# Conditioning rows moved to other stages of a two-layer trunk, and the mixer's due jobs run sooner

## The chip, the core and the metric

The kernel runs on one core of a Trainium2 chip. The metric is the device time of one execution in microseconds (us), as the median over runs. The engines are named as in the profile: PE (TensorE, matrix products), DVE (VectorE), ACT (ScalarE), POOL (GpSimd) and SP (SyncE, whose queue issues most transfers).

## What is computed

The reference is a trunk of two layers over 1024 positions of width 1024, all in fp32. Layer 0 is a Griffin block followed by a squared-ReLU MLP; then one shared K/V is computed; layer 1 is chunked attention followed by an MLP of the same form. Each norm is modulated by shift and scale, and each residual is gated, by vectors that come from one conditioning vector `c` through the matrices `ada_w` (two layers, 6 x 1024 columns) and `kv_ada_w`:

```python
def modulate(x, shift, scale):
    return x * (1 + scale[:, None, :]) + shift[:, None, :]

def recurrent_mixer(hn, w_in, conv_w, conv_b, gate_a_w, gate_a_b, gate_x_w, gate_x_b, lam, w_out):
    z = hn @ w_in
    gate, xr = jnp.split(z, 2, axis=-1)
    xr = causal_depthwise_conv(xr, conv_w, conv_b)
    y = rg_lru(xr, gate_a_w, gate_a_b, gate_x_w, gate_x_b, lam)
    return (y * jax.nn.gelu(gate)) @ w_out

def sqrelu_mlp(hn, w1, w2):
    return jnp.square(jax.nn.relu(hn @ w1)) @ w2
```

## The kernel before

**Products.** Each fp32 operand is split into a high and a low part (fp32r), and a product is three matmuls (L329, L330, L331). ACT makes the high part (L196, tiles `wh`), DVE the low one by subtraction (L200, tiles `wl`, or `s` and the second half of `wh` for half tiles). The MLPs go by a scheme of seven products on quarters in place of eight; the weights' sums for it are made by DVE or POOL (L126), those of the hidden layer by DVE (L1182), and the sums of products by DVE: L1264 in the first product, L1286 in the second, which adds into the residual stream. A block of the first product and a step of the second are 84 matmuls each.

**Stream.** A class `Stream` plans the weight stream while the program is written. Items stand in a list; SP issues their loads (L159) in list order, into a ring of seven buffers (`ws`) or into general buffers (`s`). Items become operands in list order as buffers come free. Since each engine works in program order, this list and the moments at which the planner is asked (`ws.tick`, `ws.run`, which starts the jobs that have come due) set the order on every engine.

**Conditioning rows.** One row is an item of another kind: a load of 512 KB (128 x 1024 of `ada` or `kvada`) and on DVE one multiply-and-sum with the activated conditioning vector (L362, an instruction of its own and a short one that reads the sum). 72 rows after the first ones are dealt out one by one: `some(n)` in the mixer and beside the shared K/V (through the ring), `ada_late(n)` in the MLP of layer 0 (into general buffers). Nothing needs most of them before layer 1. The MLP of layer 1 has none.

**Stages, with times of the profiled execution.** Startup to 60; the mixer's loop over 11 tiles (to about 310), in which `some` gives rows at tiles 8, 9 and 10; out-projection in four pairs of w_out loads with four rows each (330 to 459), whose operands are the stored scan results (`ygd`); the out-projection's last part in chunks, with the squares (L541, L542) and normed parts (L605, L610, L620, L623) of the next norm as jobs (to 473); MLP of layer 0, first product in blocks q = 2 to 15 with two or three rows each (to 790), the hidden layer stored to DRAM (`hid`, issued by ACT) and loaded again, then the second product in steps (790 to 1143); K/V, attention, and layer 1's MLP (first product from 1714, second from 2026). In the trace `in_w_dram` stands for all weights whose names begin with w, `hsp` for the residual stream put aside in DRAM.

Of the kernel before, what the change touches and what calls it, by code (L numbers as in the profile page):

```python
# [27 lines left out]
def _done(t):  # L28

    return [b for b in range(W // BLK) if (b * BLK + BLK - 1) // 128 == t]  # L30
# [35 lines left out]
class Stream:  # L66
# [157 lines left out]
    def at(self, d, f, *a):  # L224

        if self.timed and d:
            self.jobs.append((self.now + d, f, a))
        else:
            f(*a)
# [74 lines left out]
def trunk(ctx: ExitStack, tc: tile.TileContext, I, out, dbg=None, stop=None):  # L304
# [16 lines left out]
    def bank(shape=(128, 512)):  # L321
        cnt[0] += 1
        return pools["b"].tile(list(shape), F32, name=f"b{cnt[0]}", tag="b")

    def hs(half):
        return slice(half * HALF, (half + 1) * HALF)
# [29 lines left out]
    ws = Stream(nc, slot, whp, wsp)  # L356
# [35 lines left out]
    def some(n):  # L392
        for _ in range(n):
            if rest:
                ws.add(*rest.pop(0))

    def gate_item(bs):
        for b in bs:
            if b % 4 == 0:
                ws.add(I["gates"][b // 4], 8 * BLK)  # L400

    def w_in(*us):
        for u in us:
            ws.add(I["w_in"][u], 1024)
# [6 lines left out]
    w_in(3)  # L411
    for t in range(4, NT):
        w_in(NT + t)
        some({8: 3, 9: 2, 10: 3}.get(t, 0))
        gate_item(_done(t - 1))
        w_in(t)
    gate_item(_done(NT - 1))
# [3 lines left out]
    def yg_items(n):  # L421
        for _ in range(n):
            k = len(ygits)
            ygits.append(ws.item([(0, S, ygd[k])], [(0, HALF, True), (HALF, HALF, True)], to="a",
                                 dep=k))

    def w_out(c, j):
        kn = 4 if c else 3
        ws.add(I["w_out"][c * 4 + j][:, : kn * 256], kn * 256)

    for j in range(4):
        if j == 0:
            yg_items(3)
        w_out(0, j)
        if j == 0:
            yg_items(4)
        w_out(1, j)
        some(4)
    yg_items(4)
    for j in range(4):  # L440
        w_out(2, j)
# [10 lines left out]
    def ada_late(n):  # L452
        for _ in range(n):
            if rest:
                src, _n, use = rest.pop(0)
                ws.item([(0, 1024, src)], [], to="u", raw=False, use=use)

    def hid_item(l, what):


        (p, nm), n = what[0], len(what)
        v, p = p, p % 16
        if n == 1:
            src = hid[p][:, HID.index(nm) : HID.index(nm) + 1]
        elif what[1][0] == v:
            i, d = HID.index(nm), HID.index(what[1][1]) - HID.index(nm)
            src = hid[p][:, i : i + d + 1 : d]
        else:
            src = hid[p : p + 2, :, HID.index(nm)].rearrange("a p b -> p a b")
        it = ws.item([(0, n * HALF, src)], [(x * HALF, HALF, True) for x in range(n)], to="a")  # L470
        for x, w in enumerate(what):
            hitems[(l, *w)] = (it, x)

    def mlp_units(l):
        for f in range(4):
            ws.add(I["w1"][l][f], 1024)
        for q in range(2, 16):
            u, v = I["w1"][l][2 * q], I["w1"][l][2 * q + 1]
            ws.add_quad(u[:, :512], u[:, 512:], v[:, :512], v[:, 512:], 512, V)
            ada_late(0 if l or q == 2 else 2 if q in (3, 15) else 3)  # L480
        for s in STEPS[: 16 if l else 15]:
            def quad(s):
                c = slice(s * 128, s * 128 + 512)
                ws.add_quad(*(I["w2"][l][s % 4][x][:, c] for x in range(4)), 512,
                            G if s > 1 else V)

            if s == 0:

                for nm in NAMES:
                    hid_item(l, [(0, nm), (1, nm)])  # L490
                    hid_item(l, [(2, nm), (3, nm)])
                    if nm == "B11":
                        quad(0)
            else:
                quad(s)
            if l or s < 14:
                if s < 15:
                    for nms in HLOADS:
                        hid_item(l, [(s + 4, nm) for nm in nms])
        if l == 0:  # L500
            for e in range(2):
                ws.add(I["w2t"][e], 1024)
            hid_item(l, [(18, "B11"), (18, "B12")])
            hid_item(l, [(18, "B22"), (18, "B21")])
            hid_item(l, [(16, "B12"), (17, "B12")])
            hid_item(l, [(15, "B12")])

    mlp_units(0)

    for g in range(2):  # L510
# [8 lines left out]
    for m in range(8):  # L519
        ws.add(I["wo"][m], 1024)  # L520
    mlp_units(1)


# [564 lines left out]
    def part_of(ps, it, e, half, ys, first, last):  # L1088

        n = len(ys)  # L1090
        for k, y in enumerate(ys):
            s = slice(k * 256 + e * 128, k * 256 + e * 128 + 128)
            gh, gl = y["op"][half]
            mm3(ps, it["hi"][:, s], it["lo"][:, s], gh, gl, first and k == 0, last and k == n - 1)

    def into_h(m, half, ps):
        V.scalar_tensor_tensor(out=h[m][:, hs(half)], in0=ps, scalar=g1[:, m : m + 1],
                               in1=h[m][:, hs(half)], op0=ALU.mult, op1=ALU.add)
# [23 lines left out]
    def chunk(j, half, e):  # L1122
        m, ps = 2 * j + e, bank()
        part_of(ps, its[j], e, half, ygits[7:], True, True)
        into_h(m, half, ps)
        at(int(m < KD - 1), n2.sq, m, hs(half), int(m < KD - 2))
# [5 lines left out]
            tick()  # L1132
    for j in range(4):
        for e in range(2):
            chunk(j, 1, e)
            n = 2 * j + e
            if n == 1:
                n2.mm(0)
            elif n == 3:
                n2.bc(0)  # L1140
            elif n > 3:
                n2.mod(0, (n - 4,))
            ws.tick()
        ws.done(its[j])
# [499 lines left out]
    for n in range(N + LAG + 1):  # L1644
        if n < N:
            hd, j = todo[n]
# [148 lines left out]
```

## Time and profile before

| | us |
|---|---|
| median of 3 runs | 2350.05 (2349.6 to 2352.07) |
| profiled execution | 2351.75 |
| its span | 2350.0 |
| granted clock of PE over the span | 0.99 |
| PE busy | 2258.7 (96%) |
| DVE busy | 1751.7 (75%) |
| ACT busy | 1246.2 (53%) |
| POOL busy | 397.1 (17%) |

A busy share is a mean over stages. Which engine holds the others up in one stage is read from the waits there: the time an engine stood idle before an instruction and what released it, which the timeline puts in brackets.

### The profile page before, as it was taken

To read this page: it belongs to the slowest core of one execution; us is meant where nothing else is said; L and a number is where in the kernel's file an instruction comes from. 1 tells how busy PE (TensorE), PEld (TensorE's weight loads), DVE (VectorE), ACT (ScalarE), POOL (GpSimd) and SP (SyncE) were. 2 spreads that over 40 slices of the span, in tenths; PEclk is the share of its full clock that TensorE was granted. 3 is DMA by queue.
4 is the path that set the end of the run, shared out by engine and by line. 5 is a ranking of instruction groups with operands and counts; after the bars stand their busy time and mean duration, and the time that the engine had idled before them with its cause. 6 is when DMAs were issued, how large, how long until landed. Compare 5 with 4: busy or idle time off the path is not lost.

```text
span 2350.0 us, 29512 instructions
## 1 busy us (share of the span) xinstructions
PE 2258.7 (96%) x10588; PEld 1871.9 (80%) x10588; DVE 1751.7 (75%) x2580; ACT 1246.2 (53%) x2148; POOL 397.1 (17%) x419
## 2 busy tenths in 40 slices
PE   4999989999999899999999989999999999999999
PEld 2878768878888678888888879997888888778887
DVE  8688887698787877777774759996496655877775
ACT  5587873375555634344443249995275555633332
POOL 0001100000000033331000068873000000033332
PEclk9999999999999999999999999999999999999999
DMA  8225466426666865445244200014114444865543
GB/s 316 72 83 153 121 208 214 176 68 237 245 249 235 305 232 158 152 151 207 84 159 126 90 12 10 11 53 148 64 58 160 171 165 168 297 232 160 157 150 128
DMA packets 141631, 363.32 MB, mean 155 GB/s; under 512 B 14924, under 2 KB 17100, under 8 KB 141484
## 3 DMA queue, kind: packets, MB, share of 16 engines
q1 hardware_dynamic: 113756, 278.45, 35.3%
q10 hardware_dynamic: 23824, 71.44, 8.1%
q0 software_dynamic: 3904, 11.54, 1.9%
q8 instruction: 83, 1.36, 0.2%
q14 instruction: 64, 0.52, 0.1%
HBM read 260.19 MB, written 89.65 MB: 149 GB/s over the span
## 4 chain that ended last, share of the span: by engine, by line
PE 68%; DVE 10%; DMA 10%; ACT 6%; issue 3%; POOL 2%; ACTq 0%; SPq 0%; POOLq 0%; DVEq 0%
PE b L329 21%; PE b L330 21%; PE b L331 21%; DMA hid<-s 4%; DMA ws<-in_w_dram 3%; DMA ws<-hid 2%; DVE wl L200 2%; PE b L1601 1%; ACT s L1571 1%; DVE s L200 1%; DVE s L1182 1%; ACT s L334 1%; POOL ws L126 1%; PE b L1620 1%; PE b L1621 1%
## 5 line engine op out<-in xcount | busy, mean ns | idle before, releaser
L329 PE MATMUL b<-s,wh 128*128 128x512 f32 (+1 forms) x2532 | 999.1, 395 | 29.6 <-DVE s L1286 11.0
L330 PE MATMUL b<-s,wh 128*128 128x512 f32 (+1 forms) x2532 | 994.6, 393 | 17.1 <-DVE s L200 8.5
L331 PE MATMUL b<-s,wl 128*128 128x512 f32 x2296 | 901.0, 392 | 1.7 <-DVE wl L200 1.7
L329 PEld LDWEIGHTS b<-s,wh 128*128 128x128 f32 (+1 forms) x2532 | 477.9, 189 | 144.2 <-DVE s L1286 8.5
L330 PEld LDWEIGHTS b<-s,wh 128*128 128x128 f32 (+1 forms) x2532 | 478.0, 189 | 124.3 <-DVE s L200 10.1
L196 ACT ACTIVATE wh<-ws 128x1024 fp32r<-128x1024 f32 (+3 forms) x302 | 291.4, 975 | 480.0 <-POOL ws L126 260.4
L331 PEld LDWEIGHTS b<-s,wl 128*128 128x128 f32 x2296 | 433.2, 189 | 95.9 <-DVE wl L200 2.5
L200 DVE TENSOR_TENSOR wl<-ws,wh 128x1024 fp32r<-128x1024 f32 (+1 forms) x249 | 304.3, 1224 | 156.5 <-ACT wh L196 154.2
L200 DVE TENSOR_TENSOR s<-ws,s 128x512 fp32r<-128x512 f32 x284 | 224.8, 807 | 7.4 <-ACT s L196 7.4
L1286 DVE SCALAR_TENSOR_TENSOR s<-b,mod,s 128x512 f32<-128x512 f32 x221 | 164.7, 746 | 86.4 <-PE b L331 86.3
L126 POOL TENSOR_TENSOR ws<-ws 128x512 f32<-128x512 f32 x21 | 27.8, 1322 | 1112.0 <-DVE s L1286 467.7
L196 ACT ACTIVATE s<-ws 128x512 fp32r<-128x512 f32 x284 | 164.4, 618 | 77.6 <-DMA ws<-hid 25.1
L330 PE MATMUL b<-wl,s 128*128 128x512 f32 x384 | 149.9, 390 | 0.0
L329 PE MATMUL b<-wh,s 128*128 128x512 f32 x384 | 148.9, 389 | 0.0
L331 PE MATMUL b<-wh,s 128*128 128x512 f32 x384 | 146.4, 389 | 1.1 <-DVE s L584 1.1
L1264 DVE TENSOR_TENSOR s<-s,b 128x512 f32<-128x512 f32 x84 | 57.3, 683 | 75.3 <-PE b L331 69.0
L362 DVE CUSTOM_DVE_ANT_0 ws<-ws,cb,vec 128x1024 f32<-128x1024 f32 x59 | 75.1, 1281 | 32.8 <-DMA ws<-in_ada_dram 26.1
L1262 ACT ACTIVATE s<-b 128x512 f32<-128x512 f32 x84 | 50.0, 595 | 89.7 <-PE b L331 87.5
L331 PE MATMUL b<-s,wh 128*128 128x512 f32 x236 | 92.5, 392 | 0.0
L335 DVE TENSOR_TENSOR s<-b,s 128x384 fp32r<-128x384 f32 x144 | 82.7, 593 | 12.1 <-ACT s L334 11.6
L1576 POOL TENSOR_SCALAR s<-s,sm 128x640 f32<-128x640 f32 (+4 forms) x128 | 86.1, 685 | 22.3 <-DVE sm L1574 22.3
L1571 ACT ACTIVATE s<-s,sm 128x640 f32<-128x640 f32 (+4 forms) x128 | 88.3, 696 | 1.6 <-DVE sm L1569 1.6
(165 smaller groups left out, 2980.7 us busy)
## 6 DMA issues: line engine op xcount, KB each, us to landing
hid<-s ACTq DMA_DIRECT2D x128, 512.0 KB, 4.9
ws<-hid SPq DMA_DIRECT2D x118, 512.0 KB, 4.9
ws<-in_w_dram SPq DMA_DIRECT2D x220, 256.0 KB, 3.6
ws<-in_ada_dram SPq DMA_DIRECT2D x56, 512.0 KB, 4.4
s<-in_ada_dram SPq DMA_DIRECT2D x40, 512.0 KB, 7.9
ws<-in_w_in_dram SPq DMA_DIRECT2D x22, 512.0 KB, 7.2
hsp<-s SPq DMA_DIRECT2D x32, 256.0 KB, 2.0
s<-hsp SPq DMA_DIRECT2D x16, 512.0 KB, 7.8
```

Of the source, the lines that this page charges most:

```text
L126: eng.tensor_tensor(out=out, in0=in0, in1=in1, op=op)
L196: self.nc.scalar.activation(out=hi[:rows, :n], in_=src, func=AF.Copy)
L200: self.nc.vector.tensor_tensor(out=lo[:rows, :n], in0=src, in1=hi[:rows, :n].bitcast(F32), op=ALU.subtract)
L329: PE.matmul(ps, ah, bh, start=start, stop=False, skip_group_check=more)
L330: PE.matmul(ps, ah, bl, start=False, stop=False, skip_group_check=more)
L331: return PE.matmul(ps, al, bh, start=False, stop=stop, skip_group_check=more).ins
L335: V.tensor_tensor(out=lo, in0=src, in1=hi.bitcast(F32), op=ALU.subtract)
L362: V.tensor_tensor_reduce(out=t, in0=t, in1=cb, op0=ALU.mult, op1=ALU.add, scale=1.0, scalar=bias, accum_out=dst)
L1264: V.tensor_tensor(out=t, in0=t, in1=ps, op=ALU.add)
L1286: V.scalar_tensor_tensor(out=t, in0=ps, scalar=g2[:, m : m + 1], in1=t, op0=ALU.mult, op1=ALU.add)
L1571: A_.activation(out=p[:, lo:640], in_=p[:, lo:640], func=AF.Exp, scale=-1.0, bias=m, accum_out=s1)
L1576: G.tensor_scalar(out=p[:, lo:640], in0=p[:, lo:640], scalar1=sm[:, 4 + e : 5 + e], scalar2=1.0, op0=ALU.mult, op1=ALU.mult)
```

## The change

Five edits. In the mixer's loop the eight rows stand with tiles 6, 7 and 8 in place of 8, 9 and 10. The out-projection's four pairs get 0, 5, 5 and 6 rows in place of four each. In the first product of layer 0's MLP the blocks q = 14 and q = 15 get no rows (they had three and two). In its second product the steps 4 to 11 get one row each. The mixer's last chunks run due jobs before each chunk. The number of rows is the same, so three fewer stand beside the shared K/V. Every line after L496 moves down by one, after L1135 by two.

```diff
--- before.py
+++ after.py
@@ -411,7 +411,7 @@
     w_in(3)
     for t in range(4, NT):
         w_in(NT + t)
-        some({8: 3, 9: 2, 10: 3}.get(t, 0))
+        some({6: 3, 7: 2, 8: 3}.get(t, 0))
         gate_item(_done(t - 1))
         w_in(t)
     gate_item(_done(NT - 1))
@@ -435,7 +435,7 @@
         if j == 0:
             yg_items(4)
         w_out(1, j)
-        some(4)
+        some((0, 5, 5, 6)[j])
     yg_items(4)
     for j in range(4):
         w_out(2, j)
@@ -477,7 +477,7 @@
         for q in range(2, 16):
             u, v = I["w1"][l][2 * q], I["w1"][l][2 * q + 1]
             ws.add_quad(u[:, :512], u[:, 512:], v[:, :512], v[:, 512:], 512, V)
-            ada_late(0 if l or q == 2 else 2 if q in (3, 15) else 3)
+            ada_late(0 if l or q in (2, 14, 15) else 2 if q == 3 else 3)
         for s in STEPS[: 16 if l else 15]:
             def quad(s):
                 c = slice(s * 128, s * 128 + 512)
@@ -493,6 +493,7 @@
                         quad(0)
             else:
                 quad(s)
+            ada_late(int(l == 0 and 3 < s < 12))
             if l or s < 14:
                 if s < 15:
                     for nms in HLOADS:
@@ -1132,6 +1133,7 @@
             tick()
     for j in range(4):
         for e in range(2):
+            ws.run()
             chunk(j, 1, e)
             n = 2 * j + e
             if n == 1:
```

DVE, out-projection's first pair, from the timeline's 348.76 on; `s<-ws` are lows of stored scan results, `wl` lows of w_out, L362 rows. Before:

```order
L200 TENSOR_TENSOR s_2391<-ws_2195,s_2391 128x512
L200 TENSOR_TENSOR s_2393<-ws_2195,s_2393 128x512
L362 ISA ws_2378,mod_82<-ws_2378,cb,vec 128x1024
L362 ISA mod_82 128x1
L200 TENSOR_TENSOR s_2395<-ws_2305,s_2395 128x512
L200 TENSOR_TENSOR s_2397<-ws_2305,s_2397 128x512
L1014 TENSOR_TENSOR s_2022<-s_2022,s_2284 128x1024
L362 ISA ws_2449,mod_82<-ws_2449,cb,vec 128x1024
L362 ISA mod_82 128x1
L1097 SCALAR_TENSOR_TENSOR s_2454<-b_2464,mod_82,s_2454 128x512
```

After:

```order
L200 TENSOR_TENSOR s_2391<-ws_2195,s_2391 128x512
L200 TENSOR_TENSOR s_2393<-ws_2195,s_2393 128x512
L200 TENSOR_TENSOR s_2395<-ws_2305,s_2395 128x512
L200 TENSOR_TENSOR s_2397<-ws_2305,s_2397 128x512
L200 TENSOR_TENSOR wl_2487<-ws_2351,wh_2486 128x768
L1015 TENSOR_TENSOR s_2022<-s_2022,s_2284 128x1024
L362 ISA ws_2448,mod_82<-ws_2448,cb,vec 128x1024
L362 ISA mod_82 128x1
L1098 SCALAR_TENSOR_TENSOR s_2453<-b_2463,mod_82,s_2453 128x512
L362 ISA ws_2484,mod_82<-ws_2484,cb,vec 128x1024
```

One row (its two instructions) has gone from between the lows, a second a few instructions ahead (`ws_2351`), and a low of w_out stands sooner.

DVE, second product, the step from 874 on. Before:

```order
L1286 SCALAR_TENSOR_TENSOR s_6367<-b_6433,mod_82,s_6367 128x512
L200 TENSOR_TENSOR s_6515<-ws_6380,s_6515 128x512
L1286 SCALAR_TENSOR_TENSOR s_6367<-b_6434,mod_82,s_6367 128x512
L200 TENSOR_TENSOR wl_6532<-ws_6428,wh_6531 128x1024
L200 TENSOR_TENSOR s_6534<-ws_6380,s_6534 128x512
L1286 SCALAR_TENSOR_TENSOR s_6367<-b_6435,mod_82,s_6367 128x512
```

After:

```order
L1288 SCALAR_TENSOR_TENSOR s_6352<-b_6418,mod_82,s_6352 128x512
L200 TENSOR_TENSOR s_6502<-ws_6365,s_6502 128x512
L1288 SCALAR_TENSOR_TENSOR s_6352<-b_6419,mod_82,s_6352 128x512
L362 ISA s_6442,kvmod<-s_6442,cb,vec 128x1024
L362 ISA kvmod 128x1
L200 TENSOR_TENSOR wl_6519<-ws_6413,wh_6518 128x1024
L200 TENSOR_TENSOR s_6521<-ws_6365,s_6521 128x512
L1288 SCALAR_TENSOR_TENSOR s_6352<-b_6420,mod_82,s_6352 128x512
```

A row stands behind the second L1286 (now L1288) of the step; seven later steps read alike.

SP, second product, one of the following steps. Before:

```order
L159 DMA ws_6726<-in_w_dram 128x512
L159 DMA ws_6731<-in_w_dram 128x512
L159 DMA ws_6754<-in_w_dram 128x512 x2
L159 DMA ws_6796<-hid 128x2x512
L159 DMA ws_6798<-hid 128x2x512
L159 DMA ws_6836<-hid 128x1024
```

After:

```order
L159 DMA ws_6717<-in_w_dram 128x512
L159 DMA ws_6722<-in_w_dram 128x512
L159 DMA ws_6745<-in_w_dram 128x512 x2
L159 DMA s_6748<-in_kvada_dram 128x1024
L159 DMA ws_6789<-hid 128x2x512
L159 DMA ws_6791<-hid 128x2x512
L159 DMA ws_6830<-hid 128x1024
```

The row's load stands behind the step's loads of w2 and ahead of those of the hidden layer.

DVE, mixer's end, the last normed parts ahead of the MLP. Before:

```order
L623 TENSOR_TENSOR s_3351<-s_2454,s_3351 128x512
L200 TENSOR_TENSOR wl_3355<-ws_2985,wh_3354 128x1024
L1097 SCALAR_TENSOR_TENSOR s_2503<-b_3383,mod_82,s_2503 128x512
L542 TENSOR_TENSOR s_3102<-s_3102,s_3398 128x512
L605 SCALAR_TENSOR_TENSOR s_2460<-s_2460,aa,s_2462 128x512
L542 TENSOR_TENSOR s_3102<-s_3102,s_3403 128x512
L542 TENSOR_TENSOR s_3102<-s_3102,s_3373 128x512
L623 TENSOR_TENSOR s_3376<-s_2456,s_3376 128x512
```

After:

```order
L624 TENSOR_TENSOR s_3337<-s_2453,s_3337 128x512
L200 TENSOR_TENSOR wl_3355<-ws_3007,wh_3354 128x1024
L543 TENSOR_TENSOR s_3102<-s_3102,s_3359 128x512
L543 TENSOR_TENSOR s_3102<-s_3102,s_3385 128x512
L1098 SCALAR_TENSOR_TENSOR s_2504<-b_3391,mod_82,s_2504 128x512
L543 TENSOR_TENSOR s_3102<-s_3102,s_3406 128x512
L606 SCALAR_TENSOR_TENSOR s_2459<-s_2459,aa,s_2461 128x512
L624 TENSOR_TENSOR s_3362<-s_2455,s_3362 128x512
```

Two sums of squares (L542, now L543) stand ahead of the last addition into the stream (L1097, now L1098) in place of behind it, and one normed part (L623, now L624) comes closer to it.

## Rows read from the trace of the kernel before

**Rows 1.** The page's first part: busy time of each engine, share, instructions.

```profile
PE 2258.7 (96%) x10588; PEld 1871.9 (80%) x10588; DVE 1751.7 (75%) x2580; ACT 1246.2 (53%) x2148; POOL 397.1 (17%) x419
```

**Rows 2.** Timeline, PE: start, us, engine, line, operation, count [idle before <-releaser].

```profile
342.56 0.50 PE L330 MATMUL b<-s,wh 128*128 128x512 f32 x1 [1.81 <-DVE s L200]
...
349.47 0.79 PE L330 MATMUL b<-s,wh 128*128 128x512 f32 x1 [5.95 <-DVE s L200]
...
351.88 0.80 PE L330 MATMUL b<-s,wh 128*128 128x512 f32 x1 [0.76 <-DVE s L200]
```

**Rows 3.** Timeline, DVE, in the same stretch.

```profile
337.51 1.27 DVE L362 CUSTOM_DVE_ANT_0 ws<-ws,cb,vec 128x1024 f32<-128x1024 f32 x1
...
348.76 1.26 DVE L200 TENSOR_TENSOR s<-ws,s 128x512 fp32r<-128x512 f32 x2
349.94 1.27 DVE L362 CUSTOM_DVE_ANT_0 ws<-ws,cb,vec 128x1024 f32<-128x1024 f32 x1
351.14 0.08 DVE L362 DVE_READ_ACCUMULATOR2_ANT mod<- 128x1 f32 x1
```

**Rows 4.** Timelines, DVE and then PE, mixer's end.

```profile
473.82 0.69 DVE L542 TENSOR_TENSOR s<-s,s 128x512 f32<-128x512 f32 x1 [0.70 <-ACT s L541]
...
475.09 1.41 DVE L542 TENSOR_TENSOR s<-s,s 128x512 f32<-128x512 f32 x2
476.42 1.29 DVE L623 TENSOR_TENSOR s<-s,s 128x512 fp32r<-128x512 f32 x2
...
477.16 0.80 PE L330 MATMUL b<-s,wh 128*128 128x512 f32 x1 [3.45 <-DVE s L623]
```

**Rows 5.** Windows: us, busy (instructions) by engine, PEclk, DMA share, GB/s.

```profile
790.73:902.82 112.09, 101.54 (x421) 80.29 (x420) 90.13 (x119) 51.70 (x82) 26.01 (x16) 0.97 0.71 242
2026.27:2135.07 108.80, 100.27 (x421) 80.28 (x420) 87.81 (x118) 49.60 (x79) 25.30 (x16) 0.97 0.72 244
...
732.42:752.65 20.23, 19.34 (x85) 15.69 (x84) 18.55 (x27) 12.70 (x19) 0.00 (x0) 1.00 0.67 239
902.82:1055.14 152.32, 152.32 (x673) 126.13 (x672) 117.84 (x146) 59.90 (x91) 50.07 (x32) 1.00 0.49 152
```

**Rows 6.** Waits of PE (total, times, longest) in 640:790; PE's timeline at 877.

```profile
PE b L329 <- DVE s L1264: 1.3, 2, 0.9
...
877.76 0.50 PE L329 MATMUL b<-s,wh 128*128 128x512 f32 x1 [1.28 <-DVE s L1286]
```

**Rows 7.** Timelines of one step of the second product: DVE, SP, POOL; DVE again.

```profile
866.56 0.69 DVE L200 TENSOR_TENSOR wh<-s,wh 128x512 fp32r<-128x512 f32 x1
...
893.59 1.23 DVE L200 TENSOR_TENSOR wl<-ws,wh 128x1024 fp32r<-128x1024 f32 x1 [3.86 <-ACT wh L196]
...
884.81 2.67 SPq L159 DMA_DIRECT2D ws<-in_w_dram  x4
894.88 6.10 SPq L159 DMA_DIRECT2D ws<-hid  x3
...
891.17 1.29 POOL L126 TENSOR_TENSOR ws<-ws 128x512 f32<-128x512 f32 x1 [13.00 <-DMA ws<-in_w_dram]
...
1016.95 0.69 DVE L200 TENSOR_TENSOR wh<-s,wh 128x512 fp32r<-128x512 f32 x1
```

**Rows 8.** Timelines, DVE and then PE, mixer's gate of a middle tile.

```profile
180.57 1.22 DVE L944 TENSOR_TENSOR s<-s,s 88x1024 fp32r<-88x1024 f32 x1
...
186.96 0.40 PE L330 MATMUL b<-s,wh 88*88 88x512 f32 x1
```

**Rows 9.** DMA of 640:760, 1880:2000, 775:830 (issues: count, KB, median us to landing); SP's timeline.

```profile
ws<-in_w_dram SPq DMA_DIRECT2D x23, 256.0 KB, 4.1
...
ws<-in_w_dram SPq DMA_DIRECT2D x22, 256.0 KB, 3.1
...
DMA packets 7728, 17.80 MB, mean 324 GB/s; under 512 B 594, under 2 KB 594, under 8 KB 7724
...
721.54 1.72 SPq L159 DMA_DIRECT2D ws<-in_w_dram  x3
723.31 4.53 SPq L159 DMA_DIRECT2D s<-in_kvada_dram  x3
```

## The prediction

> **What bounds the kernel now.** The page first: TensorE (PE) is busy 96% of the span [rows 1], so an edit counts only where it shortens or adds a wait of PE. The matrix products keep their number and, but for two swaps, their order; the edits move work of VectorE (DVE) and the SP queue. Next the timeline of PE, for the waits over 0.5 us near the moved rows, and the timeline of DVE beneath each. There are three such places, and a fourth where PE waits for nothing while DVE has little to spare.
>
> *Output projection.* PE waits for lows of the scan's outputs (L200) 1.81, 5.95 and 0.76 us [rows 2]. DVE works without a gap from 335 to 352, and two conditioning rows (L362) stand in that chain [rows 3].
>
> *Mixer's end.* PE waits 3.45 us for a normed part (L623), behind L1097, squares' sums (L542) and L605 on DVE [rows 4].
>
> *MLP of layer 0, from first to second product.* The windows view gives a twin: the MLP of layer 1 does the same 421 matmuls with no conditioning rows in 108.80 us; layer 0 takes 112.09 [rows 5]. One block ahead of it, of 84 matmuls, takes 20.23 us instead of 19.04 (152.32 over eight steps), since PE waits for L1264; between 640 and 790 it does so twice, 1.3 us in all, the longest 0.9 [rows 5, 6].
>
> *Later steps of the second product.* From 902.82 to 1055.14 PE is busy throughout at full clock [rows 5], though it had waited 1.28 us for L1286 as late as 877.76 [rows 6]. DVE's "idle" of 3.86 us before a step's first wl (L200) isn't slack but latency of a ring: DVE frees buffers, SP issues in_w (884.81), GpSimd (POOL) waits for that transfer and adds (891.17), ScalarE (ACT) splits, DVE's wl runs (893.59) [rows 7]. That ring's period, from the wh split at 866.56 to the ninth one at 1016.95 eight steps on, is 150.39/8 = 18.80 us [rows 7], against PE's 152.32/8 = 19.04: PE is covered by 0.24 us a step.
>
> **The change part by part.** A row costs DVE 1.20 us: from 349.94 to the next instruction's start at 351.14 [rows 3].
>
> *Mixer loop (eight rows two tiles sooner).* Their loads pass w_in loads on SP, which wait for ring buffers. The nearest reader is L944 at 180.57, done at 181.79; its matmul stands at 186.96, 5.17 us later [rows 8]. Three of the moved rows come before it, 3 x 1.20 = 3.6 us, so the cover holds: 0. Were all five ahead, 6.0 would pass it by 0.8: bounds 0 and +0.8.
>
> *Out-projection (4,4,4,4 to 0,5,5,6).* The rows at 337.51 and 349.94 leave. The low that ends PE's first wait comes 1.2 us sooner, that wait shrinks by as much, and the second ends as much sooner. For the third, the low at 351.14 comes right behind that at 348.76, so its 0.76 us goes: -1.2 - 0.76 = -2.0. The second wait itself, 5.95 us for other work on DVE, stays. The last pair gets two rows more, 2.4 us, on DVE; the trace names no wait of PE between 352 and 473, so I take 0 for it. Bounds for the part: 0 (what is late behind them is a transfer) and -2.6, the first and third wait whole.
>
> *Squares and normed parts sooner.* Two L542 (of 1.41 at 475.09) come before L1097. One L542 waits for ACT's square of the last half, as it did (0.70 idle before 473.82), then L605, then L623 [rows 4]. The chain to L623 loses two L542, 1.3 us, of which some 0.6 come back as L1097 stands behind them: -0.7; bounds 0 and -1.3.
>
> *First product (five rows fewer).* Their work, 5 x 1.20 us on DVE, and 2.5 MB of loads go. The twin has none and takes 112.09 - 108.80 = 3.3 us less from 790.73 on [rows 5]. The block ahead loses 20.23 - 19.04 = 1.2; three rows' loads stand right behind its in_w loads (721.54, rows at 723.31) [rows 9], and the wait should go. Sum: -4.5; bounds 0 and -4.5, since the twin also lacks the rows before.
>
> That loads *behind* slow those ahead is read from two stretches: with rows behind them in_w loads land after 4.1 us, in layer 1 without rows after 3.1, while hid stores go beside both [rows 9]. So 1.0 us for three rows, 0.33 for one. The Trainium skill ("DMA: Bandwidth & Descriptors", section "Queues, rings and completion order") says otherwise: on each DMA engine, one issuing engine's descriptors are consumed in ring order, so a load behind would cost those ahead nothing. The medians 4.1 and 3.1 [rows 9] speak against it, without excluding it.
>
> *Second product (eight rows, steps 4 to 11).* On SP each load stands behind the step's four in_w loads and ahead of hid's, which come 10 us after in_w's (884.81, 894.88) [rows 7], so the load is out of their way. On DVE each row stands behind the second L1286 of the step, ahead of a wl: inside the ring, so it lengthens the period. By the mean period: 18.80 + 1.20 + 0.33 (the load behind in_w) = 20.33 us, against PE's 19.04: 1.29 x 8 = +10.3. Queued behind each row are wl, the lows and two L1286 that free PE's banks; PE waits for those. Bounds: nothing, if the idle before wl absorbs them, and 8 x (18.80 + 1.20 + 1.0 - 19.04) = +15.7 if one load delays in_w as much as three did. I take 10.3, being the ring's own mean.
>
> *Shared K/V (three rows fewer).* PE doesn't wait there: 0.
>
> Sum: -2.0 - 0.7 - 4.5 + 10.3 = +3.1 on the profiled execution's 2351.75, 2354.85. That lies 1.70 above the median 2350.05, so 2353.2 on the median. About 0.2%, 4.7 us, is what can be told from no change; this is within.
>
> **The rivals.**
> 1. *Second product's rows are hidden.* DVE stands idle 3.86 us ahead of 893.59, over the 1.20. Against it: that idle is the ring's latency, released by the DMA chain that starts with DVE. If so: 2350.05 - 7.2 = 2342.8, faster. Chance 0.15.
> 2. *Loads behind cost nothing.* Rows then cost 8 x (20.00 - 19.04) = 7.7, and the 1.2 us block stays: -2.0 - 0.7 - 3.3 + 7.7 = +1.7, 2351.8. For it: rows' loads stand behind in_w in every block of that product, yet only two waits stand in 150 us. Against it: the landings 4.1 and 3.1. Chance 0.16. The rule of the Trainium skill's page "DMA: Bandwidth & Descriptors" (same section) is this case.
> 3. *The transition doesn't get faster.* Between 775 and 830 the DMA engines move 324 GB/s on average [rows 9], with hid loads, in_w and reloads that stay. Removed row loads ended before 760. If these transfers set the end, the five rows' DVE time was beside them: -2.0 - 0.7 + 10.3 = +7.6, 2357.7, slower. It decides from where the part gives less than 2.9 us (7.6 - 4.7). Against it: layer 1 has the same transfers and 3.3 us less. Chance 0.23.
> 4. *One load delays in_w by a full 1.0 us*: +15.7 instead of 10.3, 2358.6, slower. It decides from 11.9. Chance 0.08.
>
> **How the numbers follow.** My own sum has 0.38, of which 0.04 falls beyond the bound on the slow side. Faster 0.15 (rival 1), same 0.34 + 0.16 = 0.50, slower 0.23 + 0.08 + 0.04 = 0.35. Range: at the slow end rival 4 and its bounds, 2360; at the fast end most of the way to rival 1, 2344, leaving its larger part out.
>
> **What would show it.** PE's waits at 342 to 352 should be about 0.6, 5.95 and none; that for L623 about 2.7. The 421 matmuls that took 112.09 should take about 109, plus a row's 1.3. Eight steps that took 152.32 should take about 162, with PE waiting for L1286 once or more a step and the wh splits 20.3 us apart. If these steps stay at 152, rival 1 holds; if the splits are 20.0 apart and in_w lands as before, rival 2; if the 421 matmuls still take 112 or more, rival 3. A wait in the mixer's tiles 6 to 8 would be a miss none of these price.

## The result and the profile after

The changed kernel takes 2359.81 us (median of 9 runs, 2355.58 to 2365.09), the kernel before 2350.18 beside it (9 runs): ratio 1.004, 95% interval 1.003 to 1.0049. It is slower by 9.6 us, where 2353.2 was forecast.

The table compares the same stretches of PE's matmuls, found by their order, in two executions of each kernel. Stretches are named by their times in the kernel before.

| stretch | before, twice | after, twice | predicted difference |
|---|---|---|---|
| mixer, 180 to 206 | 25.95, 25.96 | 31.96, 32.21 | 0 |
| out-projection, 330 to 380 | 49.93, 50.20 | 45.55, 45.64 | -2.0 |
| normed parts, 470 to 480 | 10.11, 10.16 | 8.26, 8.27 | -0.7 |
| first product, 480 to 862 | 381.67, 381.14 | 377.21, 378.17 | -4.5 |
| second product, 862 to 1055 | 193.26, 193.45 | 203.88, 203.68 | +10.3 |
| its last steps, 1055 to 1143 | 88.04, 88.04 | 90.45, 88.53 | 0 |

The out-projection, the normed parts and the two products went the predicted way. The mixer did not, and the last steps lost 2.4 us in one execution and 0.5 in the other.

Windows, in the columns of [rows 5]. First the mixer's stretch of before, then of after the same stretch, the out-projection, the 421 matmuls and the eight steps of [rows 5]:

```profile
179.70:205.65 25.95, 25.95 (x115) 20.59 (x114) 20.00 (x21) 23.61 (x29) 2.09 (x4) 1.00 0.56 166
```

```profile
179.82:211.78 31.96, 29.69 (x115) 22.16 (x114) 24.69 (x24) 25.41 (x30) 3.15 (x6) 0.89 0.55 162
335.84:381.39 45.55, 39.52 (x166) 30.92 (x164) 34.28 (x40) 31.71 (x39) 2.10 (x4) 0.93 0.85 302
789.64:900.05 110.41, 99.35 (x422) 79.25 (x421) 88.53 (x120) 49.39 (x78) 25.26 (x16) 0.98 0.72 247
900.05:1060.74 160.69, 154.15 (x674) 125.66 (x672) 125.60 (x158) 58.18 (x88) 50.71 (x32) 1.00 0.51 163
```

The mixer's 115 matmuls take 6.0 us more, and their granted clock fell from 1.00 to 0.89. The 421 matmuls take 110.41 instead of 112.09, and the eight steps 160.69 instead of 152.32.

PE's timeline after, three places: the mixer, the out-projection and the mixer's end. The last two answer to [rows 2, 4].

```profile
190.33 0.47 PE L329 MATMUL b<-s,wh 88*88 88x512 f32 x1 [1.00 <-ACT s L911]
...
192.92 0.72 PE L329 MATMUL b<-s,wh 88*88 88x512 f32 x1 [0.97 <-ACT s L919]
193.44 0.63 PE L330 MATMUL b<-s,wh 88*88 88x512 f32 x1
...
196.07 0.80 PE L329 MATMUL b<-s,wh 128*128 128x512 f32 x1 [0.30 <-ACT s L971]
...
353.42 0.79 PE L330 MATMUL b<-s,wh 128*128 128x512 f32 x1 [5.95 <-DVE s L200]
...
477.92 0.50 PE L330 MATMUL b<-s,wh 128*128 128x512 f32 x1 [2.96 <-DVE s L624]
```

Three waits for ACT are new in the mixer; 0.63 us a matmul (0.39 elsewhere) is the lower of the two clock levels (1.2 GHz). Of the out-projection's three waits only the middle one is left. The last is 2.96 instead of 3.45.

PE's waits in the eight steps of after (total, times, longest), and DVE's first and ninth wh split, which answer to those at 866.56 and 1016.95 [rows 7]:

```profile
PE b L329 <- DVE s L1288: 6.5, 6, 1.5
```

```profile
861.77 0.68 DVE L200 TENSOR_TENSOR wh<-s,wh 128x512 fp32r<-128x512 f32 x1
...
1025.23 0.68 DVE L200 TENSOR_TENSOR wh<-s,wh 128x512 fp32r<-128x512 f32 x1
```

The splits are (1025.23 - 861.77)/8 = 20.43 us apart; 20.33 was predicted, 18.80 it was before. PE waits six times in these eight steps, where once or more a step was expected.

### The profile page after: what moved, and what is told of

Its sections match the earlier page's. It is cut to its first block, busy times and chain, and to the rows that moved or that the text cites. A ratio compares the mean times of both kernels' runs of the same rounds, so it can differ in the third digit from the quotient of the medians.

```text
span 2360.7 us, 29496 instructions
## 1 busy us (share of the span) xinstructions
PE 2259.4 (96%) x10588; PEld 1869.5 (79%) x10588; DVE 1752.9 (74%) x2580; ACT 1248.0 (53%) x2148; POOL 398.5 (17%) x419
## 4 chain that ended last, share of the span: by engine, by line
PE 68%; DVE 10%; DMA 7%; ACT 7%; issue 4%; POOL 3%; SPq 0%; POOLq 0%; ACTq 0%; DVEq 0%
PE b L329 21%; PE b L330 21%; PE b L331 21%; DMA ws<-hid 3%; DMA ws<-in_w_dram 2%; DVE s L200 2%; DVE wl L200 2%; POOL ws L126 2%; ACT s L1573 2%; PE b L1603 1%; ACT s L334 1%; DVE s L1288 1%; ACT wh L196 1%; DMA s<-in_w_dram 1%; PE b L1622 1%
## 5 line engine op out<-in xcount | busy, mean ns | idle before, releaser
L1288 DVE SCALAR_TENSOR_TENSOR s<-b,mod,s 128x512 f32<-128x512 f32 x221 | 164.1, 743 | 65.5 <-PE b L331 65.4
L362 DVE CUSTOM_DVE_ANT_0 ws<-ws,cb,vec 128x1024 f32<-128x1024 f32 x56 | 71.1, 1278 | 30.8 <-DMA ws<-in_ada_dram 30.8
```

Source lines behind the costliest of these rows:

```text
L362: V.tensor_tensor_reduce(out=t, in0=t, in1=cb, op0=ALU.mult, op1=ALU.add, scale=1.0, scalar=bias, accum_out=dst)
L1288: V.scalar_tensor_tensor(out=t, in0=ps, scalar=g2[:, m : m + 1], in1=t, op0=ALU.mult, op1=ALU.add)
```

## The experiments

A letter for each edit: A the mixer's rows, B the out-projection's, C none in the first product's last two blocks, D eight in the second product, F the due jobs. A time has its ratio to the kernel before on the same chip behind it, with the 95% interval.

**Which edit costs? Runs 1 to 3: the changed kernel without A, without D, without both.**

```diff
-        some({6: 3, 7: 2, 8: 3}.get(t, 0))
+        some({8: 3, 9: 2, 10: 3}.get(t, 0))
```

```diff
-            ada_late(0 if l or q in (2, 14, 15) else 2 if q == 3 else 3)
+            ada_late(0 if l or q in (2, 14, 15) else 2 if q == 3 else 4 if q < 12 else 3)
...
-            ada_late(int(l == 0 and 3 < s < 12))
```

> The changed kernel, but the mixer's eight rows stand with tiles 8, 9 and 10 again. Theory (the two traces laid side by side: between 180 and 206 the changed kernel loses 6.0 us that the kernel before does not lose): the three PE waits at 190 to 196 and the slow clock behind them go, and the time falls by 6.0 from 2359.8 to about 2353.8. Rival (a gap at one place is made up elsewhere, since PE's later waits are set by DVE): 2358 or more.

> The changed kernel without rows in the second product; the eight stand in the first product's blocks q = 4 to 11, four in place of three. Theory (the ring of DVE, SP, POOL and ACT is lengthened by a row): PE's waits for L1286 in steps 5 to 12 go, and with them 13.6 us (the traces' gap grows from -5.6 at 841 to +8.0 at 1100): 2346.2. Rival (the gap came from the first product's change or from slower transfers that stay): less than 6 us are regained, 2354 or more. If four rows don't hide in a block, PE waits for L1264 near 560 to 660 and up to 8 us less is regained.

> The mixer's rows back at tiles 8 to 10 and the eight step rows in blocks q = 4 to 11: of the change, the out-projection's rows, the first product's last blocks and the jobs remain. Theory (the places add up): 2359.8 - 6.0 - 13.6 = 2340.2, faster than the kernel before by 0.4%. Rival (gains overlap): 2346 to 2350.

Without A: 2353.74 us (1.0016, 1.0005 to 1.0027). Without D: 2350.24 (1.0006, 0.9994 to 1.0018). Without both: 2344.55 (0.9978, 0.9966 to 0.9989). So A costs 2359.81 - 2353.74 = 6.1 us, or by the other pair 2350.24 - 2344.55 = 5.7. D costs 2353.74 - 2344.55 = 9.2, or 2359.81 - 2350.24 = 9.6. By the ratios, which set each kernel against the one before on its own chip, A costs 5.6 or 6.6 and D 8.9 or 8.0, so neither is known to better than a microsecond. The first run came out as expected. The other two came out 4 us above, since 13.6 had been expected of taking D back.

**Run 4: the kernel before with B and F alone.**

```diff
-        some(4)
+        some((0, 5, 5, 6)[j])
...
+            ws.run()
             chunk(j, 1, e)
```

> The kernel before with two edits alone: the out-projection's 0, 5, 5, 6 rows and the jobs run before the mixer's last chunks. Theory from the traces' gaps (4.4 at 330 to 380, 1.9 at 470 to 480): 2350.2 - 6.3 = 2343.9. By the prediction's own terms (2.0 and 0.7): 2347.5. Rival (the next stage waits for what it waited for anyway): 2350.

2346.42 us (0.9984, 0.9973 to 0.9995): -3.0. The prediction's terms, -2.0 and -0.7, hold; the larger gain that the two traces show in these stretches does not (last section).

**Run 12: the kernel before with C alone**, the five rows going to earlier blocks.

```diff
-            ada_late(0 if l or q == 2 else 2 if q in (3, 15) else 3)
+            ada_late(0 if l or q in (2, 14, 15) else 2 if q == 3 else 4 if q < 9 else 3)
```

> The kernel before with one edit: no rows in the first product's blocks 14 and 15, and one row more in each of the blocks 4 to 8. The prediction's term for that (3.3 us from layer 1's twin and 1.2 us of the block at 732) gives -4.5: 2345.0 us where the kernel before takes 2349.5. The same stretches over the traces at hand, 480 to 862 us, take 381.67, 381.14 and 379.40 us with these rows and 377.2 to 379.6, mean 378.1, without: -2.7, 2346.8. The difference of two medians that hold this edit and eight rows moved was -1.9: 2347.6.

2347.63 us against 2348.98 (0.9998, 0.9987 to 1.0008): -1.4 by the medians, -0.5 by the ratio. The interval leaves out 2345.0, so the term of -4.5 is refuted. It doesn't tell -1.4 from -2.7, or from nothing.

**How do the second product's rows cost? Runs 5 to 7**, all three with A undone, so they compare with run 1 (2353.74, with these rows) and run 3 (2344.55, without). Run 5 only lets a row wait longer before DVE takes it: behind the wh split, in the idle time ahead of a step's first wl, where the prediction had seen no slack for a row *inside* the ring.

```diff
                 if (p, x) == (15, 0):
                     ws.lag["p"] = 2
+                    ws.lag["u"] = 8
```

> Mixer's rows back at tiles 8 to 10; the eight step rows stay in the second product with their loads, but the planner holds each row four ticks longer, so that on DVE it stands behind the wh split that frees the buffers for the next in_w loads, in the stretch in which DVE waits. Theory (a row costs only where it lengthens the ring): the step's period stays at 19.04 and the time falls from 2353.7 (mixer back) to 2344 to 2347. Rival (DVE's total work, or the row's load, is what costs): 2352 to 2355 as before.

2347.95 us (0.9994, 0.9982 to 1.0007), a little above the 2344 to 2347 of its theory. DVE's timeline in run 5, one step:

```profile
920.39 0.69 DVE L200 TENSOR_TENSOR wh<-ws,wh 128x512 fp32r<-128x512 f32 x1
...
922.92 1.27 DVE L362 CUSTOM_DVE_ANT_0 s<-s,cb,vec 128x1024 f32<-128x1024 f32 x1
...
928.38 1.23 DVE L200 TENSOR_TENSOR wl<-ws,wh 128x1024 fp32r<-128x1024 f32 x1 [2.91 <-ACT wh L196]
```

The same row, a few instructions later, stands in idle time of which 2.91 us are left. Place decides, not DVE's work: 5.8 of the 9.2 us come back (2353.74 - 2347.95).

Run 6 keeps the eight loads and leaves out the sums; a copy of one column stands in their place.

```diff
-            ada_late(int(l == 0 and 3 < s < 12))
+            ada_late(int(l == 0 and 3 < s < 12), True)
...
+                if bare:
+                    use = lambda t, o=len(rest) % 16: V.tensor_copy(out=kvmod[:, o : o + 1],
+                                                                    in_=t[:, 0:1])
...
```

> Mixer's rows back; in the second product the eight rows' loads stay, but their sums are left out (a copy of one column in their place). If a load behind in_w delays in_w by 0.33 us, as the prediction had it, 8 x (18.80 + 0.1 + 0.33 - 19.04) = 1.5 us are lost against 2344.6 without these rows: about 2346. If loads behind cost nothing: 2344.6. Rival (loads are the cost): 2350 or more.

Run 7 leaves out the loads and sums the conditioning vector with itself.

```diff
-            ada_late(int(l == 0 and 3 < s < 12))
+            if l == 0 and 3 < s < 12:
+                rest.pop(0)
+                ws.item([], [], to="u", raw=False,
+                        use=lambda t, o=len(rest) % 16: V.tensor_tensor_reduce(
+                            out=t, in0=cb, in1=cb, op0=ALU.mult, op1=ALU.add, scale=1.0,
+                            scalar=vc("kvb", o), accum_out=kvmod[:, o : o + 1]))
```

> Mixer's rows back; in the second product the eight sums stay at their place on DVE, but over a tile that is there already: their loads are left out. If DVE's 1.2 us in the ring are the cost, 2344.6 + 7.7 = 2352 to 2354, as with both; if the loads are, 2344.6 to 2346.

Loads only: 2345.84 us (0.9986, 0.9971 to 1.0001), as its first theory said. Sums only: 2352.21 (1.0015, 1.0001 to 1.0029), as its first theory said. Against run 3 the loads cost 1.3 us by the medians, which the intervals don't tell from nothing, and the sums 7.7. Windows of the eight steps: runs 3, 5, 6, 7.

```profile
894.27:1046.59 152.32, 152.32 (x673) 126.13 (x672) 118.13 (x147) 60.19 (x91) 49.81 (x32) 1.00 0.48 151
```

```profile
899.81:1053.11 153.30, 152.78 (x674) 125.97 (x672) 125.14 (x160) 60.91 (x91) 49.33 (x32) 1.00 0.55 171
```

```profile
898.48:1053.10 154.62, 153.34 (x674) 125.77 (x673) 117.06 (x152) 60.01 (x91) 49.09 (x32) 1.00 0.55 169
```

```profile
902.09:1059.69 157.60, 154.12 (x673) 125.67 (x672) 124.78 (x158) 58.26 (x88) 50.77 (x32) 1.00 0.48 147
```

No row 152.32; rows behind wh 153.30; loads alone 154.62; sums alone 157.60; both 160.69. A sum inside the ring adds 1.19 us a step to the period (19.98 - 18.79): the 1.20 of [rows 3], whole. A load adds 0.59 (19.38 - 18.79).

The ring can be cut in two: from SP's issue of a step's first load of w2 to POOL's first add, which waits for them, and the rest. Means over the eight steps between the first and the ninth wh split, in us:

| kernel | period | first load to POOL's add | rest |
|---|---|---|---|
| run 3, neither | 18.79 | 6.05 | 12.74 |
| run 5, rows behind wh | 19.01 | 6.32 | 12.69 |
| run 6, loads alone | 19.38 | 6.66 | 12.72 |
| run 7, sums alone | 19.98 | 6.12 | 13.86 |
| after, both | 20.43 | 6.58 | 13.85 |

So the loads lengthen the first part and nothing else, and the sums the rest. Over all the traces the first part takes 5.94 to 6.29 us in the nine without the rows' loads in these steps and 6.32 to 6.66 in the five with them. One step, SP and then POOL, run 3 and then run 6:

```profile
895.20 1.97 SPq L159 DMA_DIRECT2D ws<-in_w_dram  x4
...
901.13 1.30 POOL L126 TENSOR_TENSOR ws<-ws 128x512 f32<-128x512 f32 x1 [12.00 <-DMA ws<-in_w_dram]
```

```profile
899.40 1.97 SPq L159 DMA_DIRECT2D ws<-in_w_dram  x4
901.47 0.38 SPq L159 DMA_DIRECT2D s<-in_kvada_dram  x1
...
906.01 1.29 POOL L126 TENSOR_TENSOR ws<-ws 128x512 f32<-128x512 f32 x1 [12.73 <-DMA ws<-in_w_dram]
```

The add stands 5.93 us behind the first issue in run 3 and 6.61 in run 6, where the row's load is queued behind the four.

**How do the mixer's rows cost? Runs 8 and 11**, with D undone, so they compare with run 2 (2350.24, with these rows) and run 3 (2344.55, mixer as before). Run 8 keeps the rows' loads and buffers at tiles 6 to 8 and leaves out the sums.

```diff
...
-                ws.add(*rest.pop(0))
+                src, w, use = rest.pop(0)
+                if bare:
+                    use = lambda t, o=16 + len(rest) % 8: V.tensor_copy(
+                        out=mods[0][:, o : o + 1], in_=t[:, 0:1])
+                ws.add(src, w, use)
...
-        some({6: 3, 7: 2, 8: 3}.get(t, 0))
+        some({6: 3, 7: 2, 8: 3}.get(t, 0), True)
...
```

> The eight step rows in the first product, the mixer's rows at tiles 6, 7 and 8 as in the change, but their sums left out (a copy of one column in their place); the loads stay. If DVE's four sums ahead of the convolution (L924 4.1 us later) cause PE's waits at 190, they go: 2344 to 2346, as with the rows back. If the loads, which stand in front of POOL's transfers, cause them: 2350, with the three waits.

Run 11 keeps the sums, in the same order on DVE, and the ring buffers, and loads nothing.

```diff
...
+                if bare:
+                    ws.item([], [], to="u", after=ws.items[-1],
+                            use=lambda t, o=16 + len(rest) % 8: V.tensor_tensor_reduce(
+                                out=t, in0=cb, in1=cb, op0=ALU.mult, op1=ALU.add, scale=1.0,
+                                scalar=vc("ab0", o), accum_out=mods[0][:, o : o + 1]))
...
```

> The changed kernel with the second product's eight rows dealt out in the first product (as in the earlier run of that kind, 2350.24 us), and of the mixer's eight rows at tiles 6 to 8 only the sums: each takes its ring buffer and its place on VectorE, but nothing is loaded, and the sum runs over the conditioning vector itself; the output of these rows is left out. In the traces the convolution of the changed kernel starts 4.1 us later (175.49 against 171.37) behind four sums, and the transfer behind it takes 4.2 us instead of 2.8, so ScalarE's L938 starts 5.5 us later (183.58 against 178.10); with the loads alone it starts 3.7 us later (181.79), all of it in the transfer, and the stretch loses 1.8 us. Theory 1, both eat one cover: with sums alone the transfer takes 2.8 us again, L938 starts 4.1 us later, at about 182.2, little after the loads-only run; the stretch of 25.95 us takes 27.8 to 28.8, TensorE stays at full clock, and the time is 2346 to 2347.5. Theory 2, the sums alone are the cause: the stretch takes 30.2 us or more with part of it at the lower clock, and the time is 2349 to 2350.5.

Loads only: 2344.97 us (0.9981, 0.9966 to 0.9995). Sums only: 2347.16 (0.9991, 0.998 to 1.0002). The stretch of 25.95 us takes 27.75 and 28.25, both at full clock. PE's waits there, run 8 and then run 11:

```profile
191.37 0.47 PE L329 MATMUL b<-s,wh 88*88 88x512 f32 x1 [0.20 <-ACT s L922]
...
193.36 0.50 PE L329 MATMUL b<-s,wh 128*128 128x512 f32 x1 [1.08 <-ACT s L974]
```

```profile
192.30 0.46 PE L329 MATMUL b<-s,wh 88*88 88x512 f32 x1 [0.22 <-ACT s L925]
194.30 0.50 PE L329 MATMUL b<-s,wh 128*128 128x512 f32 x1 [1.07 <-ACT s L977]
```

In this stretch either half alone costs 1.8 to 2.3 us, and together they cost 6.0 to 6.4; by the medians, 0.4 and 2.6 against 5.7. One execution with the mixer's rows as before (run 6) also shows a wait for ACT there, of 0.65 us, and 26.90 in place of 25.95, so half of run 8's 1.8 can come without any moved row. Theory 1 of run 11 holds: both eat one cover. One point of it was wrong: with no row loaded, it still took 5.5 us instead of 2.8 from the convolution's end to ACT's split, most of it the transfer, so it isn't the rows' bytes that slow it (next section).

**Runs 9 and 10: one more execution of the kernel before and of the changed one**, for what differs between executions without any edit.

> The kernel before, profiled once more. The prediction took 3.3 us at the passage from the first to the second product from one execution. If that is the kernel's own, the 421 matmuls from the first step on take 112 us again; if it is one execution's draw, they take 109.5 to 111, as in the kernel with the out-projection's rows and the jobs alone, which has the same rows there.

> The changed kernel, profiled once more. Theory: the 6 us between 180 and 206 and the 8 us between the fifth and the twelfth step are there again, to within half a microsecond and 1.5; the 2.8 us near 1400 in the attention, which two other kernels show and the rest don't, comes or goes.

2351.5 and 2359.53 us. The first table and the last section use them.

## Why the prediction was right or wrong

**The mixer's term, 0, failed; measured +5.7 to +6.1.** Two things in that step were wrong. It took three of the eight rows to stand ahead of the reader, and it looked for the cover at one reader alone. DVE's timeline ahead of the convolution, after and then before:

```profile
171.96 1.26 DVE L362 CUSTOM_DVE_ANT_0 ws<-ws,cb,vec 128x1024 f32<-128x1024 f32 x1
...
174.28 1.27 DVE L362 CUSTOM_DVE_ANT_0 ws<-ws,cb,vec 128x1024 f32<-128x1024 f32 x1
...
175.49 3.91 DVE L924 SCALAR_TENSOR_TENSOR s<-s,vec,s 128x1023 f32<-128x1023 f32 x3
```

```profile
171.37 3.91 DVE L923 SCALAR_TENSOR_TENSOR s<-s,vec,s 128x1023 f32<-128x1023 f32 x3
```

Four rows (two more at 142.41 and 155.36) stand in a chain with little slack (DVE idles 2.0 us in it, 2.4 before), and the convolution starts 4.1 us later. Behind it POOL issues copies of its result, and ACT splits them. ACT's timeline, after and then before:

```profile
183.58 1.06 ACT L938 ACTIVATE s<-s 88x1024 fp32r<-88x1024 f32 x1 [9.76 <-DMA s<-s]
187.31 1.06 ACT L938 ACTIVATE s<-s 88x1024 fp32r<-88x1024 f32 x1 [2.67 <-DMA s<-s]
188.39 1.28 ACT L911 ACT_TABLE_LOAD   x1
189.68 1.09 ACT L911 ACTIVATE s<-b 128x512 f32<-128x512 f32 x2
```

```profile
178.10 1.06 ACT L937 ACTIVATE s<-s 88x1024 fp32r<-88x1024 f32 x1 [3.96 <-DMA s<-s]
181.92 1.06 ACT L937 ACTIVATE s<-s 88x1024 fp32r<-88x1024 f32 x1 [2.76 <-DMA s<-s]
...
184.29 1.09 ACT L910 ACTIVATE s<-b 128x512 f32<-128x512 f32 x2
```

The prediction followed the split to its consumer on DVE (L944), 5.17 us ahead of its matmul [rows 8]. In this trace that cover held, with 0.7 us left (L945 is done at 185.91, the matmul stands at 186.63). In the two other traces with the same rows in the mixer it did not: PE waits 0.70 us for it in run 2 and 0.79 in run 10. PE's timeline in run 10:

```profile
188.31 0.47 PE L330 MATMUL b<-s,wh 88*88 88x512 f32 x1 [0.79 <-DVE s L945]
...
193.66 0.46 PE L329 MATMUL b<-s,wh 88*88 88x512 f32 x1 [0.97 <-ACT s L919]
...
196.81 0.79 PE L329 MATMUL b<-s,wh 128*128 128x512 f32 x1 [0.41 <-ACT s L971]
```

That wait is of the size of the prediction's bound of +0.8. The larger part came by another way. ACT takes its instructions in order, and behind the two splits stand those that empty PE's banks (L911 to L971, `s<-b`). They come 5.4 us later, and PE waits for them, 1.00, 0.97 and 0.30 us. A late instruction also delays what is queued behind it, and that queue wasn't read. The Trainium skill ("PSUM — Partial Sum Buffer", section "Engine vs sequencer instructions") calls ScalarE's queue a strict FIFO; the rows agree, the table load at 188.39 following the split that ended at 188.37.

The copies took longer for a reason that the prediction had named and priced at nothing: w_in loads wait for ring buffers. From the convolution's end to the first split it takes 4.2 us, before 2.8. SP's timeline, before and then after; windows from 175 to 184 of before, run 11 and after:

```profile
163.78 0.33 SPq L159 DMA_DIRECT2D ws<-in_w_in_dram  x1
```

```profile
175.16 2.33 SPq L159 DMA_DIRECT2D ws<-in_w_in_dram  x2
```

```profile
175.00:184.00 9.00, 9.00 (x41) 7.45 (x40) 7.71 (x8) 3.12 (x3) 1.04 (x2) 1.00 0.51 134
```

```profile
175.00:184.00 9.00, 9.00 (x41) 7.44 (x41) 8.86 (x10) 0.00 (x0) 1.04 (x2) 1.00 0.87 245
```

```profile
175.00:184.00 9.00, 9.00 (x41) 7.44 (x41) 8.89 (x9) 0.42 (x1) 1.05 (x2) 1.00 0.97 274
```

With the rows in the ring the w_in loads go out at 175.16 and move beside the copies (DMA share 0.97, before 0.51). Run 11 has no row loads but the rows' buffers, and the w_in loads stand there too (174.42): share 0.87, 5.5 us from the convolution's end to the split. In run 8 the convolution starts as before (171.54), the w_in loads go out at 171.97 and 173.39 (share 0.88), and it takes 6.3 us. That the shared DMA engines are what stretches the copies is read from this coincidence; no run moved the w_in loads alone.

The waits of after sum to 2.27 us, but the stretch loses 6.0. Most of the rest is clock: matmuls at 0.63 us from 193.44 to 199.23. In runs 8 and 11, with 1.3 us of waits, the granted clock stayed at 1.00. So the two halves, 1.8 and 2.3, give more than their sum.

**The out-projection and the jobs, -2.7, were right: -3.0 in run 4.** The first wait was predicted at 0.6 and is 0.66 in run 4, 0.60 to 1.40 in three other runs with B, none in after; the second stayed at 5.95; the third went; that for L623 was predicted at 2.7 and is 2.96 to 2.97.

**The first product's term, -4.5, failed: -1.4 in run 12 (which can be nothing), -1.9 as the difference of runs 3 and 4, which also deal out eight rows differently.** The block at 732 did as predicted: 19.04 us in every kernel with C, 20.23, 20.47 and 19.96 in those without. The 3.3 us behind it came from one execution of each layer [rows 5]. Over all the traces layer 1's twin takes 108.24 to 110.03 us, and layer 0's stretch with rows 112.09, 111.17 and 110.69, so the pair at hand was nearly the widest one. In run 12 the 421 matmuls take 112.75 us, more than the 112.09 and 111.17 of before, so what the block gains is lost again behind it: 480 to 862 takes 381.15, before 381.67 and 381.14. The sign that the prediction gave, about 109 plus a row's 1.3, seemed met by the 110.41 of the first trace after; the second execution took 111.95, so that was luck. This is rival 3 in the main: the transition's end isn't set by the rows' work. Whether the transfers set it, as that rival said, is not shown.

**The second product's term, +10.3, was right in mechanism and nearly in size: 9.2 to 9.6.** The period of the ring was the right quantity. For sums alone the prediction's numbers give 18.80 + 1.20 = 20.00, and run 7 shows 19.98; for both, 20.33 and 20.43. Rival 1 falls for the place that the change chose; run 5 shows it true of another place, a few instructions later. Rival 2, that loads behind cost nothing, falls by the ring's period: run 6 has the loads alone, and POOL's add comes 0.61 us later after the first issue (6.66 against 6.05). PE's cover of 0.24 us a step takes up part of it, and 8 x (19.38 - 19.04) = 2.7 us are left, against 2.3 in the window. So a price for a load behind was right in kind and too small: 0.33 in the prediction, 0.5 to 0.6 measured inside the ring. But its source doesn't carry it. The medians of landings, 4.1 and 3.1, came from other stretches, and such medians can't tell. The DMA issues between the first and the ninth wh split (count, KB, median us to landing), the kernel before, run 3 and run 6:

```profile
ws<-in_w_dram SPq DMA_DIRECT2D x26, 256.0 KB, 3.6
```

```profile
ws<-in_w_dram SPq DMA_DIRECT2D x26, 256.0 KB, 2.7
```

```profile
ws<-in_w_dram SPq DMA_DIRECT2D x26, 256.0 KB, 2.8
```

Neither before nor run 3 has a row's load there, and still they show 3.6 and 2.7, while run 6, with the loads, shows 2.8. A landing stands in the trace for only some of the four loads of a step, and POOL waits for the last of them. The Trainium skill ("DMA: Bandwidth & Descriptors", section "Queues, rings and completion order") says that each DMA engine consumes descriptors in ring order, and adds that a later one may finish its write before an earlier one. That a load behind would then cost nothing was the prediction's own conclusion, and run 6 speaks against it. How the load behind holds up those ahead is open. Rival 4, a full 1.0 us for each load, falls (it would give a period of 21.0).

**The sum.** By medians B and F give -3.0, C -1.4 to -1.9, D +9.2 to +9.6, A +5.7 to +6.1: together +10.0 to +11.3, against the +9.6 measured, which the intervals cover. The forecast's +3.1 missed mainly by the mixer's 6 and the first product's 3, and +9.6 is more than the 4.7 us that the prediction took for no change. The range's slow end, 2360, had been built from rival 4 and the second product's bounds, not from these terms; that 2359.81 still lies inside it is luck. The prediction had said that a wait in the mixer's tiles 6 to 8 would be a miss that it hadn't priced, and it was that. Run 3, which leaves out A and D and keeps the rest, beats both kernels with 2344.55 us.

## What to carry to other kernels

When an instruction comes later, look behind it on its own queue as well as at its consumer: here an in-order engine held the emptying of PE's banks behind a split. Work put onto a busy engine is free or costs its whole length by its place in the ring that sets the period, a few instructions apart, so price it per place and not by the engine's busy share. A wait for several transfers ends with the last one, so time it from the issue to the waiting instruction and not by a median of landings. A difference between two stretches of one execution needs a second execution before it becomes a term.

## What the runs showed of the hardware

After waits of the same length, the clock came back at different times. PE's timeline behind the out-projection's wait, in run 4 and run 12, and at the mixer's end in run 12:

```profile
349.42 0.80 PE L330 MATMUL b<-s,wh 128*128 128x512 f32 x1 [5.94 <-DVE s L200]
```

```profile
350.02 0.80 PE L330 MATMUL b<-s,wh 128*128 128x512 f32 x1 [5.94 <-DVE s L200]
...
476.54 0.50 PE L330 MATMUL b<-s,wh 128*128 128x512 f32 x1 [3.45 <-DVE s L623]
```

Behind 5.94 or 5.95 us of idle, the matmuls at 0.63 us (the lower level, 1.2 GHz) number 6 in the traces of after and run 3, 7 in run 12, 12 in runs 4 and 5, and 13 in both of before. Behind the same 3.45 us they number 5 in before and none in run 12, with the same instructions around it. So the out-projection's stretch, with its rows as before, takes 49.93 and 50.20 us in the traces of before but 48.20 in run 12; with B it takes 45.37 to 48.01. The mixer's end takes 10.11 and 10.16 but 8.81 in run 12; with F, 8.24 to 9.69. That is why the traces of after show -4.4 and -1.9 there while run 4 gains 3.0 in all. What sets the moment of the return, the runs don't tell. Two stretches that no edit touches move alike: 1390 to 1420 takes some 29.1 to 32.6 us over the traces, and 1600 to 1700 takes 97.05 to 99.82.
